# Input projection weights of the second sequence split into high and low parts by transfers from GpSimd's queue

## The chip, the cores and the metric

The kernel runs on one core of one Trainium2 chip. The metric is the device time of one execution in microseconds; the time before is the median of three runs. One further execution was taken with the hardware profiler, and the views quoted here come from it. Engine names: PE is TensorE (matmuls; PEld its weight loads), DVE is VectorE, ACT is ScalarE, POOL is GpSimd, SP is SyncE.

## What is computed

One encoder layer is applied to two inputs, a sequence of 512 tokens and one of 1024, each of width 1024. A normalized input is projected by one wide matrix `w_in` into everything that the two token mixers need; the mixers' outputs are gated, merged and projected, and a SwiGLU FFN follows. Cut to what matters here:

```python
h = rms_norm(x, n_pre_mix)
proj = h @ w_in
qkv_g, z_g, a_g, b_g, q_h, f_h, i_h, g_h, gate_raw = jnp.split(proj, IN_SPLITS, axis=-1)
...
o_a = gated_delta_chunked(q, k, v, g[0], beta[0]) + flip_seq(gated_delta_chunked(...))
o_b = gla_chunked(qh, kh[0], ih, logf[0]) + flip_seq(gla_chunked(...))
...
merged = gates[:, :, 0] * y_a + gates[:, :, 1] * y_b
x = x + rms_norm(merged @ w_out, n_post_mix)
h2 = rms_norm(x, n_pre_ffn)
ff = (jax.nn.silu(h2 @ w_gate) * (h2 @ w_up)) @ w_down
return x + rms_norm(ff, n_post_ffn)
```

All is float32. Both sequences use the same weights.

## The kernel before

**Precision by parts.** A float32 product is made of three TensorE products in the shorter format `float32r`: every operand is written as a high part (the value rounded to `float32r`) and a low part (the value less the high part), and `mm3` adds high x high, high x low and low x high in one PSUM bank. So every weight that arrives must first be split. `split` (line 836) does it with two instructions: ACT copies the raw weights to the high part, and DVE subtracts the high part from the raw ones and writes the low part.

**Input weights.** `w_in` is cut into blocks of 128 output columns, 512 KB each, laid out as 128 partitions x 1024 values. `fetch` (line 1268) loads a block from SP's queue into a raw tile of the general work space (pool `big`), `split_w` makes the two parts in a pair of slots of the weight pool (`NW` slots of 1024 values; 6 before), and `in_w` (line 1263) joins the two. The blocks used by a sequence are q, k and v of the delta-rule mixer for four heads, six blocks a head for the other mixer and the branch gates z and G (`dense`), and 16 blocks of the merging gates (`gates`). `proj` (line 1233) multiplies one block with one 512-token block of the input in 24 matmuls of 128 x 512; the first sequence has one such token block, the second has two.

**Order of the work.** The kernel's text isn't issued as it stands. Generators for the parts of the layer (`pre_stream`, `gdn_stream`, `hg_stream`, `dense_stream`, `p2_stream`) are interleaved by a first planner (`Plan.run`), which walks TensorE's time; `TOKENS` and `NORMED` are planner times at which the start's normalization may go on, and `take_w` and `give_w` hold two weight tokens. The operations that come out are recorded on a `Tape`, and `Tape.schedule` puts them in order a second time for each engine: it charges each an occupancy (`occ`) and a duration (`dur`) by `Tape.cost`, adds `SLACK` to results that cross from one engine to another, allows eight transfers in flight (`LANES`), looks at most `AHEAD` = 500 operations ahead of the earliest one unfinished, gives out tiles as they come free, and prefers operations that `sooner` has moved forward. What comes out is a fixed order of instructions for each engine's queue; on the chip the engines wait for each other by semaphores alone.

**POOL's own work in the second sequence.** `inverse` (line 1339) runs 31 steps of two small operations, each needing the one before, on POOL; its result goes through a scratch tensor in DRAM to `merges`, whose small matmuls (32 x 32, then 64 x 64) PE does; then `gdn_mix` steps through the recurrence. POOL issues no transfers.

Of the kernel before, what the change touches and what calls it, by code (L numbers as in the profile page):

```python
# [33 lines left out]
C_Z, C_A, C_QH, C_FH, C_IH, C_GH, C_GATE = 1536, 2048, 2064, 2576, 3600, 4112, 4624  # L34
QSCALE = 128.0 ** -0.5
TBUFS = 8
NW = 6
NH = NFF // 2
MIXER = ("ones", "offd", "m_all", "m_b", "mbd", "wab0", "wab1")
RBUFS = 1  # L40
# [7 lines left out]
NVEC = 88  # L48
AHEAD = {0: 1536, 1: 2064, 4: 4112 - 512}
TRIG = 2  # L50
TOKENS, NORMED = 10.0, 30.0
QSQ = P * EPS ** 0.5
EPSQ = P * EPS * EPS

# [108 lines left out]
class Tape:  # L163
# [12 lines left out]
    AHEAD = 500  # L176
    RATE = 260.0
    FETCH = 5000.0
    BLOCK = 256
    SLACK = {"sync": 600, "vector": 100, "scalar": 100, "gpsimd": 100, "tensor": 100}  # L180

# [106 lines left out]
    def cost(self, o, out, ins, scal):  # L288
        e, m = o.eng, o.meth
        n = self.free_size(out)  # L290

        def psum(a):
            v = self.vts.get(a.tensor.name)
            return v is not None and v.pool.kind == "PSUM"
        if m == "dma_start":
            vo = self.vts.get(out.tensor.name)
            run = self.row(out, ins[0])
            rows = out.shape[0] * n // run
            o.form = rows * max(run * 4, 512) / self.RATE
            if vo is None or vo.pool.kind == "DRAM":  # L300
                o.dur = 1200.0
            elif [x for x in ins[0].ap if x[0] == 0 and x[1] > 1]:
                o.dur = 4000.0
            else:
                o.dur = 2000.0
            o.occ = 380.0 if rows < 512 else 450.0
            if o.dur < 2000.0 and run < P:
                o.occ = 600.0
            return
        if e == "tensor":  # L310
            if m == "transpose":
                o.occ = 110
                o.form = self.FULL
            else:
                k = self.free_size(ins[1])
                form = (ins[0].shape[0], self.free_size(ins[0]))
                if ins[1].dtype == F32R:
                    o.occ = k / 2.4 + 13.5
                else:
                    o.occ = 2 * (2 * k / 2.4 + 5.5) if k > 32 else 24  # L320
                    o.form = form
                    if form == (64, 64):
                        o.occ = 62
                    elif form == (P, 32) and k > 32:
                        o.occ = 32 if k <= 64 else k / 2.4 + 3
            o.dur = o.occ + 165
            return
        if e == "scalar":
            d = 200 + 0.84 * self.free_size(ins[0]) - (45 if psum(ins[0]) else 0) + 92 * len(scal)
            o.dur, o.occ = d, d - (95 if o.kw.get("accum_out") is None else 0)  # L330
            return
        if e == "vector":
            ps = psum(out) or any(psum(i) for i in ins)
            if not ps and m != "memset" and (m != "tensor_scalar" or n > 1):
                o.port = 138 + 65 * len(scal)
            if m == "tensor_tensor_scan":
                d = 155 + 1.98 * n
            elif m in ("tensor_copy", "tensor_scalar", "memset") and not ps:
                d = 145 + 0.53 * n
            else:  # L340
                d = 145 + 1.055 * n
            if m in ("copy_predicated", "transpose"):
                d += 30
            d += 65 * len(scal)
            o.dur, o.occ = d, d - 75
            return
        if m == "memset":
            d = 90 + 0.86 * n
        elif m == "affine_select":
            d = 100 + 1.05 * n  # L350
        else:
            d = 192 + (1.87 if n < TB else 2.15) * n
        if m != "memset":
            o.port = 138
        o.dur, o.occ = d, d - 40
# [79 lines left out]
    def schedule(self):  # L435
# [33 lines left out]
        def lat(a, b):  # L469
            a, b = self.ENGS[a], self.ENGS[b]  # L470
            return self.LAT.get((b, a), 30 if a == b else 36)
# [22 lines left out]
        def enable(o, t):  # L494
            o = o.unit[0]
            npend[o.idx] -= 1
            o.rel = max(o.rel, t)
            if npend[o.idx] == 0:
                ask(o)
# [14 lines left out]
        while done < len(ops):  # L514
# [69 lines left out]
            for o in o.unit:  # L584
                start[o.idx] = (t, done)
                turn[o.idx] = (first, done)
                for v in o.tiles:
                    if v.pool.kind == "PSUM":
                        v.use[e] = t + o.dur
                done += 1  # L590
                clock[e] = t + o.occ
                fin = t + o.dur
                for s in o.succ:
                    if s.eng == e == "tensor":
                        enable(s, t + o.occ)
                    else:
                        enable(s, fin + lat(e, s.eng) + (self.SLACK[e] if e != s.eng else 0))
                for v in o.tiles:
                    if v.left == len(v.ops):
                        v.fin = {}  # L600
                    v.left -= 1
                    v.fin[e] = max(v.fin.get(e, 0.0), fin)
                    if v.left == 0:
                        v.pool.give(v)
                        if v.pool not in freed:
                            freed.append(v.pool)
                t += o.occ
# [157 lines left out]
def layer(ctx, tc, x_p, x_s, w_out, n_post_mix, n_post_ffn, w_down, vec, xt_p, xt_s, w_in, w_br, w_gate, w_up,  # L765
# [196 lines left out]
    def whl():  # L962
        return [pl.tile(wsp, [P, 1024], F32R, n, n, WBUFS[i]) for i, n in enumerate(("whi", "wlo"), 1)]

    def split_w(raw, kt, m):
# [3 lines left out]
            split(hi[:, 0:n], lo[:, 0:n], raw[:, 0:n])  # L969
        return [v[:, 0:n].rearrange("p (k m) -> p k m", m=m) for v in (hi, lo)]  # L970

    def get_w(src, kt, m):
        raw = raw_w()
        if kt * m == src.shape[1]:
            dma(raw, src)
        else:
            dma(raw.rearrange("p (k m) -> p k m", m=m), src.rearrange("(k p) m -> p k m", p=P))
        return split_w(raw, kt, m)
# [281 lines left out]
                give_w()  # L1260
            yield 0

    def in_w(c0):
        return split_w(ahead.pop(c0) if c0 in ahead else fetch(c0), KD, P)

    ahead = {}
# [99 lines left out]
    def gdn_in(q, h, out):  # L1366
        nb = q.nb
        out.update({"ktok": {}, "vtok": {}, "q2": {}, 0: {}, 1: {}, "D": {}, "vc": {}, "nrm": {}})
        yield take_w(True)
        w = in_w(512 + h * P)  # L1370
        for b in range(nb):
            for d in range(2):
                dm = gt_("at", 4)
                dma(dm, q.cr[4 * d + h:4 * d + h + 1, b * TB:(b + 1) * TB].to_broadcast([P, TB]))
                sg = 1 if d == 0 else -1
                nc.gpsimd.affine_select(t4(dm), t4(dm), [[0, 4], [sg, P]], ALU.is_ge, NEG, base=0,
                                        channel_multiplier=-sg)
                pl.op("POOL", dm, [dm])
                out["D"][b, d] = dm
        yield pl.at(w[1])  # L1380
        yield from conv_proj(q, h, 1, w, out)
        while out["post"]:
            yield from out["post"].pop(0)

    def qv_in(q, h, out):
        for pi in (0, 2):
            yield take_w(True)
            w = in_w(pi * 512 + h * P)
            yield pl.at(w[1])
            yield from conv_proj(q, h, pi, w, out)  # L1390

# [325 lines left out]
    def dense_stream():  # L1717
        for q in seqs:
            lists = [list(dense(q)), list(gates(q))]
            yield need(("h", q.si, 0))  # L1720

            def pick():
                for l in lists:
                    if l and need(*l[0][0])() is not None:
                        return l.pop(0)
                return None

            def avail():
                for l in lists:
                    if l and need(*l[0][0])() is not None:  # L1730
                        return 0.0
                return None
            cur = None
            while lists[0] or lists[1] or cur:
                if cur is None:
                    yield avail
                    yield take_w(False)
                    it = pick()
                    cur = (it, in_w(it[1]))
                    yield None  # L1740
                nxt = None
                if tok["w"] and not tok["want"] and avail() is not None:
                    tok["w"] -= 1
                    it = pick()
                    nxt = (it, in_w(it[1]))
                it, w = cur
                yield from proj(q, w, it[2])
                if it[3] and waiting:
                    waiting.append(lambda k=it[3]: pl.mark(k))
                elif it[3]:  # L1750
                    pl.mark(it[3])
                cur = nxt
            pl.mark(("dense", q.si))
# [875 lines left out]
```

## Time and profile before

| | |
|---|---|
| median of 3 runs | 2383.68 us (2383.06 to 2385.79) |
| the profiled execution, whole | 2382.66 us |
| its span, first to last instruction | 2381.0 us |
| transfers | 337.72 MB, mean 142 GB/s |
| reads of HBM | 254.59 MB |

The profile gives the busy time of each engine, and for a stretch of time the same by engine. An operation's row ends with the engine's idle time just before it and what ended that. The chain of waits goes back from the last instruction: at each step to what released it, or to the instruction before it on its engine. Matmuls are pipelined, and the profile lets one last until its result is out, so neighbours overlap; the pace is counted by how many start in a stretch.

### The profile page before, as it was taken

The numbers are of one execution on the slowest core, as the hardware profiler recorded it, in microseconds if no ns is written. First come the engines' busy times: TensorE is split into PE (matmuls) and PEld (weight loads), VectorE is DVE, ScalarE is ACT, GpSimd is POOL, SyncE is SP. The second block draws the span as 40 slices with busy tenths as digits, with TensorE's granted clock in tenths as the row PEclk, the third lists the DMA queues.
The fourth block names the chain that finished last, engine by engine and source line by source line (L and its number), as shares of the span: only waits on it lengthen the run. The fifth ranks groups of instructions, "written<-read, shape, count | busy, mean of one in ns | idle before, by whom it ended". The sixth has DMA issues, their size and how long they took to land.

```text
span 2381.0 us, 37933 instructions
## 1 busy us (share of the span) xinstructions
PE 2362.8 (99%) x14183; PEld 1974.6 (83%) x14183; DVE 1727.0 (73%) x2826; ACT 1239.0 (52%) x2159; POOL 755.4 (32%) x1019
## 2 busy tenths in 40 slices
PE   8999999999999999999999999999999999999998
PEld 7888888888888888888888888888888888888887
DVE  8777898857857968758766984755887877544566
ACT  6656776746637547548442464545354444433343
POOL 0623435241602612502310011114666774200221
PEclk9999999999999999999999999999999999999999
DMA  5242643221330321324873463552454544674463
GB/s 199 95 145 63 218 143 101 95 66 46 101 96 18 100 83 54 96 78 148 299 261 133 159 221 110 163 170 84 168 192 175 187 170 160 213 246 137 148 206 125
DMA packets 193496, 337.72 MB, mean 142 GB/s; under 512 B 53185, under 2 KB 92961, under 8 KB 193313
## 3 DMA queue, kind: packets, MB, share of 16 engines
q1 hardware_dynamic: 193312, 335.31, 42.6%
q8 instruction: 111, 1.82, 0.3%
q14 instruction: 73, 0.59, 0.1%
HBM read 254.59 MB, written 80.66 MB: 141 GB/s over the span
## 4 chain that ended last, share of the span: by engine, by line
PE 90%; DVE 2%; DMA 1%; ACT 1%; SPq 0%; issue 0%; POOL 0%; DVEq 0%; ACTq 0%; POOLq 0%
PE bank L649 90%; DVE la_a L649 1%; DMA ba_a<-lay_w_in 1%; DVE ba_a L649 1%; ACT la_a L649 0%; SPq L649 0%; DMA ba_a<-x_sample 0%; DVE wa_a L649 0%; ACT ba_a L649 0%; ACT wa_a L649 0%; DMA dram_g_sc<-la_a 0%; ACT sm_a L649 0%; DMA la_a<-dram_u_sc 0%; DVE sm_a L649 0%; POOL la_a L649 0%
## 5 line engine op out<-in xcount | busy, mean ns | idle before, releaser
L649 PE MATMUL bank<-ha_a,wa_a 128*128 128x512 f32 x5424 | 1307.7, 395 | 8.4 <-ACT wa_a L649 8.0
L649 PEld LDWEIGHTS bank<-ha_a,wa_a 128*128 128x128 f32 x5424 | 1003.7, 188 | 210.1 <-ACT wa_a L649 8.0
L649 PE MATMUL bank<-xr_a 128*128 128x512 f32 x1386 | 314.3, 389 | 0.0
L649 PEld LDWEIGHTS bank<-xr_a 128*128 128x128 f32 x1386 | 260.1, 188 | 54.0
L649 PE MATMUL bank<-xr_a,ha_a 128*128 128x512 f32 x1200 | 275.3, 389 | 0.0
L649 PEld LDWEIGHTS bank<-xr_a,ha_a 128*128 128x128 f32 x1200 | 225.2, 188 | 46.8
L649 POOL TENSOR_TENSOR ba_a<-ba_a 128x512 f32<-128x512 f32 (+1 forms) x123 | 159.8, 1305 | 219.0 <-ACT wa_a L649 79.9
L649 ACT ACTIVATE la_a<-la_a 128x512 f32<-128x512 f32 (+1 forms) x307 | 194.4, 649 | 42.5 <-DVE la_a L649 30.7
L649 DVE TENSOR_TENSOR wa_a<-la_a,wa_a 128x1024 fp32r<-128x1024 f32 (+1 forms) x121 | 142.0, 1184 | 59.7 <-PE bank L649 28.3
L649 ACT ACTIVATE wa_a<-la_a 128x1024 fp32r<-128x1024 f32 (+1 forms) x121 | 118.3, 986 | 106.2 <-PE bank L649 97.7
L649 DVE TENSOR_TENSOR wa_a<-ba_a,wa_a 128x1024 fp32r<-128x1024 f32 (+1 forms) x103 | 123.6, 1218 | 68.7 <-PE bank L649 57.5
L649 ACT ACTIVATE wa_a<-ba_a 128x1024 fp32r<-128x1024 f32 (+1 forms) x103 | 99.3, 980 | 118.5 <-PE bank L649 94.9
L649 ACT ACTIVATE ha_a<-ba_a 128x512 fp32r<-128x512 f32 (+1 forms) x126 | 80.7, 642 | 135.7 <-PE bank L649 109.9
L649 POOL TENSOR_TENSOR la_a<-la_a 128x256 f32<-128x256 f32 (+1 forms) x80 | 89.4, 1133 | 183.1 <-DVE la_a L649 67.9
L649 DVE TENSOR_TENSOR ha_a<-ba_a,ha_a 128x512 fp32r<-128x512 f32 (+1 forms) x126 | 127.9, 1020 | 13.4 <-ACT ha_a L649 12.8
L649 DVE TENSOR_TENSOR la_a<-la_a 128x512 f32<-128x512 f32 (+2 forms) x193 | 126.2, 669 | 12.6 <-ACT la_a L649 11.6
L649 POOL TENSOR_TENSOR la_a<-la_a,sm_a 128x30 f32<-128x30 f32 (+43 forms) x248 | 124.6, 502 | 18.3
L649 POOL TENSOR_TENSOR sm_a<-la_a 128x126 f32<-128x126 f32 (+37 forms) x155 | 79.8, 515 | 133.2 <-DMA la_a<-dram_u_sc 104.4
L649 PE MATMUL bank<-wa_a,ha_a 128*128 128x512 f32 x528 | 120.1, 389 | 0.0
L649 DVE TENSOR_TENSOR xr_a<-da_a,xr_a 128x1024 fp32r<-128x1024 f32 (+2 forms) x60 | 71.2, 1200 | 64.1 <-ACT xr_a L649 44.0
L649 ACT ACTIVATE ba_a<-ba_a 128x512 f32<-128x512 f32 (+1 forms) x164 | 104.6, 648 | 24.0 <-DVE ba_a L649 16.7
L649 PEld LDWEIGHTS bank<-wa_a,ha_a 128*128 128x128 f32 x528 | 99.0, 188 | 20.5
(205 smaller groups left out, 3305.0 us busy)
## 6 DMA issues: line engine op xcount, KB each, us to landing
la_a<-lay_w_in SPq DMA_DIRECT2D x67, 512.0 KB
ba_a<-lay_w_in SPq DMA_DIRECT2D x37, 512.0 KB
ba_a<-lay_w_gate SPq DMA_DIRECT2D x35, 512.0 KB
ba_a<-lay_w_up SPq DMA_DIRECT2D x34, 512.0 KB
dram_a_sc<-xa_a SPq DMA_DIRECT2D x56, 256.0 KB
ba_a<-w_ffn_down SPq DMA_DIRECT2D x24, 512.0 KB
da_a<-dram_a_sc SPq DMA_DIRECT2D x22, 512.0 KB
ba_a<-dram_a_sc SPq DMA_DIRECT2D x20, 512.0 KB
```

Of the source, the lines that this page charges most:

```text
L649: f(*[m(a) for a in o.args], **{k: m(a) for k, a in o.kw.items()})
```

## The change

For the second sequence (`q.si` is 1) `in_w` no longer loads raw weights and splits them. `cast_w` issues a transfer from POOL's queue that casts the weights from DRAM to `float32r` in the high tile; ACT writes minus the high part to the low tile; and a second transfer from POOL's queue adds the weights from DRAM to the low tile. No raw tile and no DVE instruction is left. These operations are moved forward by `CAST` = 150 places (the split had `URGENT` = 100).

Beside that, the weight pool gets 8 slots for 6, `TOKENS` is 14 for 10, the second planner charges a transfer from POOL 1300 ns of POOL's time and 2600 ns plus its bytes (twice for one that adds), and it adds the slack of SP's transfers behind every transfer, those whose user is on the same queue too.

```diff
-NW = 6
+NW = 8
+CAST = 150
-TOKENS, NORMED = 10.0, 30.0
+TOKENS, NORMED = 14.0, 30.0
+    ISSUE = 1300.0
...
+            if e == "gpsimd":
+                o.dur = 2600.0
+                o.occ = self.ISSUE
+                if o.kw:
+                    o.form *= 2
+                return
...
-                        enable(s, fin + lat(e, s.eng) + (self.SLACK[e] if e != s.eng else 0))
+                        enable(s, fin + lat(e, s.eng) + (self.SLACK["sync" if o.meth == "dma_start" else e] if e != s.eng or o.meth == "dma_start" else 0))
...
+    def cast_w(src):
+        hi, lo = whl()
+        with nc.sooner(CAST):
+            nc.gpsimd.dma_start(hi, src)
+            pl.dma(hi, src)
+            act(lo, hi.bitcast(F32), AF.Copy, scale=-1.0)
+            nc.gpsimd.dma_start(lo, src, accum_op=ALU.add)
+            pl.dma(lo, src)
+        return [v.rearrange("p (k m) -> p k m", m=P) for v in (hi, lo)]
...
-    def in_w(c0):
+    def in_w(q, c0):
+        if q.si:
+            return cast_w(w_in[(c0 if c0 < C_A else c0 - (C_QH - C_A)) // P])
         return split_w(ahead.pop(c0) if c0 in ahead else fetch(c0), KD, P)
```

The four calls of `in_w` pass `q` along.

More of the change, by code (lines that the diff above doesn't have):

```diff
@@ L1369, in gdn_in @@
         yield take_w(True)
-        w = in_w(512 + h * P)
+        w = in_w(q, 512 + h * P)
         for b in range(nb):
@@ L1387, in qv_in @@
             yield take_w(True)
-            w = in_w(pi * 512 + h * P)
+            w = in_w(q, pi * 512 + h * P)
             yield pl.at(w[1])
@@ L1738, in dense_stream @@
                     it = pick()
-                    cur = (it, in_w(it[1]))
+                    cur = (it, in_w(q, it[1]))
                     yield None
@@ L1744, in dense_stream @@
                     it = pick()
-                    nxt = (it, in_w(it[1]))
+                    nxt = (it, in_w(q, it[1]))
                 it, w = cur
```

## The prediction

> **What bounds the kernel now.** I read the page's first part, then the stages, then TensorE's waits, then the chain that ended last.
>
> ```profile
> span 2381.0 us, 37933 instructions
> PE 2362.8 (99%) x14183; PEld 1974.6 (83%) x14183; DVE 1727.0 (73%) x2826; ACT 1239.0 (52%) x2159; POOL 755.4 (32%) x1019
> ```
>
> TensorE (PE) lacks 18.2 us of being busy all the time. Where these lie is shown by the stages: 0 to 390 us is the first sequence's mixer, 390 to 1060 us the second sequence's projections, recurrences and gates, where the changed weights are used, 1060 to 1662 us the merge and the first part of the FFN, and the rest the FFN's end. The columns are PE, weight loads, VectorE (DVE), ScalarE (ACT), GpSimd (POOL), the granted clock, the transfer engines' busy share and GB/s.
>
> ```profile
> 0.00:390.00 390.00, 379.91 (x2759) 315.09 (x2760) 315.88 (x598) 266.76 (x486) 157.81 (x359) 1.00 0.41 137
> 390.00:1060.00 670.00, 669.31 (x5252) 567.68 (x5251) 500.14 (x967) 386.90 (x734) 212.20 (x382) 1.00 0.27 80
> 1060.00:1662.00 602.00, 602.00 (x3038) 502.97 (x3037) 418.75 (x657) 292.69 (x479) 99.77 (x91) 1.00 0.51 173
> 1662.00:2381.00 719.00, 711.55 (x3140) 588.85 (x3138) 492.23 (x605) 292.69 (x463) 285.62 (x188) 1.00 0.52 176
> ```
>
> In the stage that the change is about, PE is idle for 670.00 - 669.31 = 0.69 us. The idle time of the whole kernel is 10.09 us before 390, 0.69 us here and 7.45 us at the end, behind the last matmul. PE's waits, and the last pieces of the chain, say the same:
>
> ```profile
> PE bank L649 <- ACT wa_a L649: 9.1, 4, 8.0
> PE bank L649 <- DVE la_a L649: 0.6, 1, 0.6
> PE bank L649 <- DVE wa_a L649: 0.4, 1, 0.4
> ...
> 404.38 240.51 PE bank L649 x1749
> 644.90 182.99 PE bank L649 x1329
> 827.93 1545.63 PE bank L649 x7897
> 2373.59 0.70 DVE da_a L649
> ```
>
> One wait of 8.0 us is the start; from 404.38 to 2373.56 the chain is PE, with two pieces of about 0.01 and 0.04 us missing between. The clock is 1.00 in every stage. So the kernel is bound by TensorE's own work, and no weight of the second sequence is waited for. What the change relieves (DVE) is busy 500.14 of 670 us and holds nothing up for long.
>
> **What it removes.** Each sequence uses 4 x 9 + 16 = 52 input weights (q, k, v and six dense blocks a head, and 16 gate blocks), so half of the 67 + 37 loads below go:
>
> ```profile
> L649 SPq DMA_DIRECT2D la_a<-lay_w_in x67: 327/423/1607, 1.7 to 1021.4; - x67
> L649 SPq DMA_DIRECT2D ba_a<-lay_w_in x37: 328/423/1336, 12.8 to 1020.4; - x37
> L649 DVE TENSOR_TENSOR wa_a<-la_a,wa_a 128x1024 fp32r<-128x1024 f32 x34 | 42.6, 1262 | 15.2 <-ACT wa_a L649 10.0 <-PE bank L649 5.2
> L649 DVE TENSOR_TENSOR wa_a<-ba_a,wa_a 128x1024 fp32r<-128x1024 f32 x13 | 16.4, 1271 | 7.3 <-PE bank L649 6.3 <-DMA la_a<-dram_w_sc 0.9
> L649 ACT ACTIVATE wa_a<-la_a 128x1024 fp32r<-128x1024 f32 x35 | 37.1, 1060 | 32.1 <-PE bank L649 29.1 <-DMA la_a<-lay_w_in 3.0
> ```
>
> (The last three rows are of 390 to 1060 us.) 52 issues of 0.42 us leave SyncE's queue, 22 us, and what stood behind them there can go earlier; 52 subtractions of 1.26 us leave DVE, 66 us; the raw tiles leave the work space. On PE's path this is worth at most the stage's 0.69 us. ACT keeps its 52 operations of 1.06 us: the copy to the high part becomes a negation of the same shape.
>
> **What it adds.** 104 transfers issued on POOL's queue, which has issued none so far, so their cost has no row. The nearest is SyncE's issue, 0.33 to 1.61 us: 104 of them take 34 to 167 us of a POOL that is free for 670 - 212.20 = 458 us. I take 1.3 us, which the new planner assumes, 135 us in all; it lies inside these ends.
>
> The transfers also move twice the bytes: 52 x 0.52 MB = 27 MB more over 670 us, 41 GB/s on top of 80. What PE does beside much more is shown by the first row here; the second gives PE's plain pace, 60 us / 266 = 0.2256 us a matmul.
>
> ```profile
> 1140.00:1200.00 60.00, 60.00 (x288) 50.44 (x287) 49.48 (x61) 24.41 (x37) 21.70 (x13) 1.00 0.80 277
> 1320.00:1380.00 60.00, 60.00 (x266) 49.70 (x265) 51.04 (x59) 25.16 (x30) 0.00 (x0) 1.00 0.47 153
> ```
>
> At 277 GB/s PE misses nothing, so the extra traffic costs nothing.
>
> **How late a weight comes.** It is now load, negate, add the load, one after the other. A lone load (issued at 735.74; nothing moves from 739 on, so it takes under 3.3 us) and the slowest piece of the chain bound one transfer:
>
> ```profile
> 735.74 0.38 SPq L649 DMA_DIRECT2D la_a<-lay_w_in  x1
> ...
> 739.00:741.00 2.00, 2.00 (x11) 1.65 (x10) 2.00 (x3) 2.00 (x5) 1.57 (x5) 1.00 0.00 0
> ...
> 246.16 7.99 DMA ba_a<-x_sample
> ```
>
> Low: 2 x 3.3 + 1.06 + 2 x 0.42 = 8.5 us. High: 2 x 7.99 + 1.06 + 2 x 1.61 = 20.3 us. Against this stands what PE has in hand. A weight feeds 2 blocks x 24 = 48 matmuls, 48 x 0.2256 = 10.8 us, and in this stage one is used up every 670 / 52 = 12.9 us. With 8 slots (NW) there is room for four pairs: three weights ahead, 32 us, beat 20.3; and four slots turn over in (20.3 + 10.8) / 4 = 7.8 us a weight, beneath 12.9. So lateness is hidden by the projections already loaded, at either end of the range. Without that cover each weight would cost up to 20.3 us, 52 times. I take 0.
>
> **Who queues behind the new waits.** The negation waits at the head of ACT's queue for the cast to land; behind it stand evictions of PSUM, and behind those PE, with eight banks of 5.4 us (24 x 0.2256) each. ACT is free for 283 of 670 us. The adding transfer waits on POOL for the negation; behind it stands the 32-step inverse of the delta rule, whose result PE's merges need. This is where it can go wrong, and is priced below.
>
> **The planner's other edits.** Instructions are put in order by a planner at build time, so NW, the later start of the norms (TOKENS 14), the 0.6 us added behind every transfer and the priorities move instructions, and add none. Ahead of 390 us they could win the idle 10.09 us less the start's 8.0, 2.1 us, and at the start
>
> ```profile
> 6.40 0.61 ACT L649 ACTIVATE la_a<-la_a 128x512 f32<-128x512 f32 x1
> 6.92 1.04 ACT L649 ACTIVATE wa_a<-la_a 128x1024 fp32r<-128x1024 f32 x1
> ```
>
> the 0.6 us of a square that ACT runs ahead of the first weight's copy. They could as well lose as much in a new order; later norms keep more projections waiting in PSUM. I take 0 between -2.7 and +2.7.
>
> **The sum.** The profiled execution took 2382.66 us, its span 2381.0 and 1.66 around it; the median, 2383.68, lies 1.02 above. On PE: nothing added, nothing removed, at most 0.69 us of waits gone. From the median: 2383.68 - 0.69 = 2383.0 us. A measurement of this kernel can tell about 0.2%, 4.8 us, from no change, so this is "the same".
>
> **Rival 1: slower, POOL holds up the inverse.** Before, for one head of the second sequence and for one of the first (POOL's first and last operation of an inverse, then PE's first merge; POOL's last, then PE's merge):
>
> ```profile
> 459.82 0.40 POOL L649 TENSOR_TENSOR sm_a<-la_a 128x31 f32<-128x31 f32 x1 [40.19 <-DMA la_a<-dram_u_sc]
> 494.96 0.24 POOL L649 TENSOR_TENSOR la_a<-la_a,sm_a 128x16 f32<-128x16 f32 x1
> ...
> 509.33 0.21 PE L649 MATMUL bank<-la_a,ba_a 32*32 32x32 f32 x1
> ...
> 107.67 0.21 POOL L649 TENSOR_TENSOR la_a<-la_a,sm_a 128x8 f32<-128x8 f32 x1
> ...
> 116.59 0.21 PE L649 MATMUL bank<-ba_a,la_a 32*32 32x32 f32 x1
> ```
>
> The inverse takes 35.4 us, and PE's merge comes 14.1 us behind it, where 8.7 sufficed in the first sequence: 5.4 us to spare. Into 35.4 us fall 35.4 / 12.9 = 2.7 weights, 5.5 issues. The new order allows 1.3 us for each; PE's order is fixed, so PE stands still once POOL loses 5.4 / 5.5 = 1.0 us more on each, that is from 2.3 us an issue. At 3.0 us the loss is (3.0 - 2.3) x 5.5 = 3.9 us a head, 15.4 us in four: 2399. For it speaks that POOL's operations do stretch beside a busy DVE, two of one shape here by three:
>
> ```profile
> 410.84 2.03 POOL L649 TENSOR_SCALAR_AFFINE_SELECT ba_a<-ba_a 128x512 f32<-128x512 f32 x1 [4.51 <-DMA ba_a<-dram_cr_sc]
> 413.52 0.68 POOL L649 TENSOR_SCALAR_AFFINE_SELECT la_a<-la_a 128x512 f32<-128x512 f32 x1 [0.65 <-DMA la_a<-dram_cr_sc]
> ```
>
> 1.3 us stretched by 2.03 / 0.68 would be 3.9. Against it: DVE has 66 us less to do, and a planner that reckons with a longer POOL also moves the merges back. The same loss would come from casts that land later than planned, with the addition stuck behind them.
>
> The Trainium skill, page "SBUF — State Buffer", speaks against the change: by its section "Who interferes with whom", a transfer issued from GpSimd has its descriptors written by GpSimd, which cannot write them while VectorE runs a copy or scalar operation in its two-port mode; its section "A bandwidth-pool intuition that's wrong" has such a transfer at 3.1 us in place of 0.62. By that, on every issue, the sum would be (3.1 - 2.3) x 5.5 x 4 = 17.6 us above no change, about 2401, an estimate from that page. But the operations it names are few in the stage; the largest such group is
>
> ```profile
> L649 DVE TENSOR_SCALAR la_a<-la_a,sa_a 128x512 f32<-128x512 f32 x22 | 12.4, 562 | 0.0
> ```
>
> 12.4 of 670 us, 2% of the time; by that share the rule would hit 2 of 104 issues and leave the time where it is. No row here shows an issue from POOL.
>
> **Rival 2: faster.** The visible waits give 0.69 + 2.1 + 0.6 = 3.4 us, 2380.3, still within 0.2%. More must come out of PE's busy time, from changes between full matmuls and small ones:
>
> ```profile
> 1033.73 4.37 PE L649 MATMUL bank<-ha_a,wa_a 128*128 128x512 f32 x18
> 1038.04 0.27 PE L649 MATMUL bank<-ba_a 64*64 64x64 f32 x1
> ```
>
> 18 matmuls take 4.31 us, where 18 x 0.2256 = 4.06: a change costs 0.25 us. An order with 16 fewer of them gives 4 us more, 2376.3. For it: weights that are ready early and a freer DVE leave the planner more full matmuls to choose from. Against it: the changes follow the steps of the merges and the recurrence, which stay.
>
> **Rival 3: the change doesn't do what it says.** If the cast left the raw bits as they are, the low part would be raw minus raw, and the same instructions would run in the same time; this belongs to the forecast's case.
>
> **Numbers.** The forecast, PE bound and all of it hidden: 0.58. Rival 1 or its like, slower by over 4.8 us: 0.26. Rival 2, faster by over 4.8 us: 0.16. The likeliest time is 2383.0. The range goes to rival 2's 2376 and rival 1's 2399, the price at 3.0 us an issue; I leave out some 0.07 below and 0.10 above, where POOL loses still more. The forecast's own range is 2380.3 to 2386.4 (0.69 and 2.7 us either way).
>
> **What would show it.** Right: PE at 669 or more of 670 us in the second sequence's stage; 52 loads fewer on SyncE; POOL with 104 issues of about 1.3 us; DVE about 66 us less busy in all; ACT unchanged; PE's waits still led by the start's 8 us. Wrong: PE idle ahead of the 32 x 32 merges with POOL as the releaser (rival 1), or on a transfer into the weight tiles (a chain longer than 32 us); or a PE busy time below 2360 us (rival 2). The forecast falls if PE's idle time outside the two ends exceeds 7 us.

## The result, and the profile after

The changed kernel takes 2392.62 us (median of 7 runs, 2391.13 to 2396.2), the kernel before 2384.05 us in runs beside them (7 runs, 2382.88 to 2385.79): 1.0037 times as long, 95% interval 1.0025 to 1.0049. So it is slower by some 9 us, where "the same", 2383.0, was forecast; 2392.62 lies inside the range. The profiled execution took 2392.4 us.

The page of after, its span, its busy times and the row of POOL's issues; then the stages, in the columns of before:

```profile
span 2390.7 us, 37932 instructions
PE 2365.8 (99%) x14183; PEld 1975.5 (83%) x14183; DVE 1667.5 (70%) x2773; ACT 1240.4 (52%) x2159; POOL 793.8 (33%) x1123
...
L657 POOL DMA_DIRECT2D wa_a<-lay_w_in x104 | 77.0, 748 | 302.3 <-PE bank L657 147.8
...
wa_a<-lay_w_in POOLq DMA_DIRECT2D x104, 512.0 KB, 5.5
...
la_a<-lay_w_in SPq DMA_DIRECT2D x36, 512.0 KB, 4.9
```

```profile
390.00:1060.00 670.00, 663.37 (x5206) 561.23 (x5205) 441.24 (x915) 384.09 (x727) 248.48 (x477) 1.00 0.49 114
1060.00:1662.00 602.00, 600.55 (x3037) 501.55 (x3036) 411.92 (x649) 286.90 (x470) 104.13 (x95) 1.00 0.53 179
1662.00:2390.70 728.70, 721.32 (x3183) 597.14 (x3181) 498.87 (x614) 300.15 (x475) 288.49 (x189) 1.00 0.51 174
```

The span is 9.7 us longer. PE's idle time went from 18.2 to 24.9 us, and its busy time from 2362.8 to 2365.8 us (2361.9 us in the kernel below that has no holds). The idle time is new in two places: 6.63 us in the second sequence's stage, where it was 0.69, and 1.45 us in the next, where it was none. What the change was to do, it did: DVE is busy 59.5 us less, and POOL issues 104 transfers. PE's waits, and pieces of the chain that ended last in the stretch that had been all PE:

```profile
PE bank L657 <- ACT wa_a L657: 9.4, 3, 8.0
PE bank L657 <- DVE la_a L657: 3.6, 3, 2.9
PE bank L657 <- issue: 1.3, 1, 1.3
PE bank L657 <- ACT la_a L657: 1.2, 2, 1.0
```

```profile
513.96 5.46 DVE ba_a L657 x5
520.97 1.66 DVE la_a L657 x2
522.76 49.96 PE bank L657 x429
...
1088.03 1.77 DVE la_a L657 x5
1089.83 3.89 DVE la_a L657 x2
1095.76 228.32 PE bank L657 x1272
```

The start's 8.0 us is as before. What is new is a wait of 2.9 us for DVE, an engine that has less work than before. The chain names the place: five DVE operations from 513.96 take 5.46 us. The instructions there, in order of time (DVE's, then POOL's, then PE's; the value behind the start is the length):

```profile
515.66 3.70 DVE L657 TENSOR_TENSOR_SCAN ba_a<-sm_a,ba_a 128x128 f32<-128x128 f32 x1
519.28 0.66 DVE L657 TENSOR_TENSOR ba_a<-la_a,ba_a 128x512 f32<-128x512 f32 x1
...
514.66 1.45 POOL L657 DMA_DIRECT2D wa_a<-lay_w_in  x2
515.83 0.93 POOL L657 TENSOR_SCALAR_AFFINE_SELECT la_a<-la_a 128x512 f32<-128x512 f32 x1
516.42 0.92 POOL L657 TENSOR_SCALAR_AFFINE_SELECT ba_a<-ba_a 128x512 f32<-128x512 f32 x1
517.02 0.89 POOL L657 TENSOR_TENSOR la_a<-la_a 128x256 f32<-128x256 f32 x1
517.60 1.48 POOL L657 TENSOR_SCALAR_AFFINE_SELECT la_a<-la_a 128x512 f32<-128x512 f32 x2
519.51 0.91 POOL L657 TENSOR_TENSOR ba_a<-ba_a 128x256 f32<-128x256 f32 x1 [0.44 <-DVE ba_a L657]
...
522.76 0.64 PE L657 MATMUL bank<-la_a 32*32 32x32 f32 x39 [2.91 <-DVE la_a L657]
```

One scan of 128x128 lasts 3.70 us; 28 others of that shape, on other tiles, take 0.41 on average (all 66 others between 390 and 1130 us: 0.44). It starts while POOL's two issues run, and ends when POOL, after two issues and five operations with no gap between them, comes to its first idle time (the 0.44 us ahead of 519.51). Behind it in DVE's queue stands what PE's 32 x 32 merge needs, and PE idles 2.91 us.

Such places can be counted: DVE operations between 390 and 1130 us that last over 1 us longer than the lower quartile of their shape ("held" from here on). Before has none; its largest excess is 0.46 us. After has six, with 11.9 us of excess together: at 398.54, 515.66, 598.03, 749.55, 917.74 and 1090.43 us. Five of them start within 1.4 us of an issue from POOL; of these, four end when POOL's run does, and the one at 398.54 ends in the middle of POOL's run, as its next issue ends. The sixth, at 598.03, is the smallest (1.19 us, 1.03 too long). It starts 6.8 us behind the last issue, and POOL had a gap of 2.74 us in between, so an issue doesn't explain it. Before has runs of POOL operations as long and as tight (four additions from 1073.01 to 1078.24, without a gap), and beside them no DVE operation loses over 0.43 us.

### The profile page after: what moved, and what is told of

The parts are those of the page before. It is cut to its first block, busy times and chain, and to the rows that moved or that the text cites. A ratio compares the mean times of both kernels' runs of the same rounds, so it can differ in the third digit from the quotient of the medians.

```text
span 2390.7 us, 37932 instructions
## 1 busy us (share of the span) xinstructions
PE 2365.8 (99%) x14183; PEld 1975.5 (83%) x14183; DVE 1667.5 (70%) x2773; ACT 1240.4 (52%) x2159; POOL 793.8 (33%) x1123
## 4 chain that ended last, share of the span: by engine, by line
PE 90%; DVE 5%; ACT 2%; DMA 2%; issue 1%; SPq 0%; POOL 0%; DVEq 0%; POOLq 0%; ACTq 0%
PE bank L657 90%; DVE la_a L657 2%; DVE ba_a L657 2%; ACT la_a L657 1%; ACT ba_a L657 1%; DVE sm_a L657 1%; DMA la_a<-lay_w_in 0%; ACT wa_a L657 0%; DMA la_a<-x_sample 0%; DMA la_a<-dram_u_sc 0%; DMA la_a<-dram_cr_sc 0%; DVE wa_a L657 0%; DMA dram_g_sc<-ba_a 0%; SPq L657 0%; ACT sm_a L657 0%
## 5 line engine op out<-in xcount | busy, mean ns | idle before, releaser
L657 POOL TENSOR_TENSOR ba_a<-ba_a 128x512 f32<-128x512 f32 (+1 forms) x130 | 170.9, 1323 | 218.2 <-DVE ba_a L657 54.6
L657 POOL DMA_DIRECT2D wa_a<-lay_w_in x104 | 77.0, 748 | 302.3 <-PE bank L657 147.8
L657 ACT ACTIVATE ha_a<-ba_a 128x512 fp32r<-128x512 f32 (+1 forms) x134 | 86.5, 650 | 147.2 <-PE bank L657 118.2
L657 ACT ACTIVATE wa_a<-ba_a 128x1024 fp32r<-128x1024 f32 (+1 forms) x88 | 81.6, 944 | 123.1 <-PE bank L657 119.7
L657 DVE TENSOR_TENSOR ha_a<-ba_a,ha_a 128x512 fp32r<-128x512 f32 (+1 forms) x134 | 134.2, 1007 | 13.3 <-ACT ha_a L657 13.2
L657 DVE TENSOR_TENSOR wa_a<-la_a,wa_a 128x1024 fp32r<-128x1024 f32 (+1 forms) x84 | 96.9, 1163 | 54.4 <-issue 22.9
L657 DVE TENSOR_TENSOR wa_a<-ba_a,wa_a 128x1024 fp32r<-128x1024 f32 (+1 forms) x88 | 98.2, 1119 | 35.8 <-PE bank L657 27.5
L657 ACT ACTIVATE wa_a<-la_a 128x1024 fp32r<-128x1024 f32 (+1 forms) x84 | 80.9, 977 | 65.5 <-PE bank L657 57.6
L657 ACT ACTIVATE xr_a<-da_a 128x1024 fp32r<-128x1024 f32 (+2 forms) x60 | 58.5, 987 | 106.0 <-PE bank L657 105.8
L657 POOL TENSOR_TENSOR sm_a<-la_a 128x28 f32<-128x28 f32 (+32 forms) x155 | 69.9, 451 | 130.9 <-DMA la_a<-dram_u_sc 120.4
```

Of the source, the lines that this page charges most:

```text
L657: f(*[m(a) for a in o.args], **{k: m(a) for k, a in o.kw.items()})
```

## The experiments

**Theory.** From the moment POOL issues a transfer, a DVE operation on SBUF can lose its turn and wait until POOL next has a gap; without an issue the two take turns, one operation each. Where POOL has a run of work behind an issue, DVE stands still for all of it, and in this kernel PE then waits for DVE. **Rivals:** the new order (slots, TOKENS, slack) costs the time; the weights land too late; the planner's wrong price of an issue, 1.3 us for a measured 0.75, packs POOL's work too tightly.

The table holds all kernels of the layer; each ratio is to runs of before on the same chip. Held and idle are those of the one profiled execution; idle is PE's, in us, in the stages 390 to 1060 and 1060 to 1662.

| kernel | median us | to before, 95% interval | held | idle |
|---|---|---|---|---|
| before | 2384.05 | | 0 | 0.69, 0.00 |
| after | 2392.62 | 1.0037 (1.0025 to 1.0049) | 6 | 6.63, 1.45 |
| planners' edits alone | 2383.52 | 0.9998 (0.9989 to 1.0007) | 0 | 2.43, 0.00 |
| transfers alone | 2392.91 | 1.0035 (1.0021 to 1.0049) | 5 | 6.34, 0.93 |
| issue at 650 ns | 2390.39 | 1.0024 (1.0015 to 1.0034) | 6 | 6.97, 0.94 |
| transfers earlier | 2393.13 | 1.0040 (1.0027 to 1.0054) | 4 | 6.29, 0.93 |
| gap, buffers moved | 2392.44 | 1.0039 (1.0026 to 1.0052) | 0 | 1.51, 0.52 |
| no gap, buffers moved | 2401.83 | 1.0073 (1.0061 to 1.0086) | 5 | 6.37, 1.56 |
| before, buffers moved | 2393.94 | 1.0040 (1.0024 to 1.0055) | 0 | 0.19, 0.00 |
| gap, buffers in place | 2382.07 | 0.9991 (0.9982 to 1.0000) | 0 | 1.20, 0.52 |
| no gap, buffers in place | 2390.66 | 1.0029 (1.0017 to 1.0040) | 6 | 5.77, 1.57 |
| gap in place, 1000 ns | 2386.26 | 1.0008 (0.9999 to 1.0017) | 0 | 1.99, 1.06 |

**Which half of the change.** The planners' edits alone:

```diff
-NW = 6
+NW = 8
-TOKENS, NORMED = 10.0, 30.0
+TOKENS, NORMED = 14.0, 30.0
...
-(self.SLACK[e] if e != s.eng else 0)
+(self.SLACK["sync" if o.meth == "dma_start" else e] if e != s.eng or o.meth == "dma_start" else 0)
```

> The planners' edits alone (8 weight slots, TOKENS 14, the longer slack behind transfers); the weights are split by ACT and DVE as before, and POOL issues no transfer. First theory (POOL's issues hold DVE back): no DVE operation between 390 and 1130 us is stretched by over 1 us, and the time stays within 3 us of before, about 2384. Rival (the new order itself costs the time): about 2392, with PE idle some 5 us or more between 390 and 1060.

And the transfers alone, which is after with these three lines put back:

> The transfers from POOL alone, with 6 weight slots, TOKENS 10 and the old slack rule. First theory (POOL's issues hold DVE back): several DVE operations stretched by over 1 us again, 2389 to 2396. Rival (the new order of slots and slack costs the time): within 3 us of before, about 2384. Third theory (the weights land too late through POOL's queue): with fewer slots the loads start later, so more than after, over 2395, with PE waiting for ACT or POOL on the weight tiles.

The edits alone give 2383.52 us, no hold, and the time of before. The transfers alone give all of the loss, 2392.91 us with five holds. The planners' edits as a cause fall. The transfers bring an order of their own, though; the gap trial below keeps that order and settles it. Lateness in the form it was given falls too, as fewer slots cost nothing on top. A kernel with after's order and the 104 transfers issued from SyncE was planned but has no measurement, so in the layer itself the issuing queue alone was never exchanged.

**The hold by itself.** A kernel of stages: both engines start together, DVE runs 24 small additions, POOL issues a transfer and runs six additions.

```python
nc.gpsimd.dma_start(hi, src)
for r in range(24):
    nc.vector.tensor_tensor(dv[r % 2], da, db, ALU.add)
for r in range(6):
    nc.gpsimd.tensor_tensor(pv[r % 2], pa, pb, ALU.add)
```

> Nothing of the layer is computed; ten short stages, each with 24 DVE additions of 128x128 beside 6 POOL additions of 128x256 without a gap, ahead of which stand: nothing, a casting transfer from POOL, the same and a small memset, a plain transfer, an adding one, two casting ones, a casting one and a wait for DVE, a casting one with no additions behind it, one between the second and third addition, and a transfer from SP. First theory, form a (any run of POOL without a gap holds DVE): in all stages with six additions, that with no transfer too, one DVE addition lasts as long as the run, 4 us or more. Form b (an issue from POOL makes it): with no transfer and with SP's no DVE addition lasts over about 1.3 us, one POOL addition and its own 0.3; in the stages with an issue just ahead one lasts to the end of the run, 3 to 5 us; behind the wait none. Rival (DVE is not held by POOL's issues): no addition over 1.3 us in any stage.

The DVE addition that stands beside POOL's run, in the stage with no transfer, with a first casting one, with a plain one, and with one between the second and third addition:

```profile
3.18 0.81 DVE L102 TENSOR_TENSOR dv<-da,db 128x128 f32<-128x128 f32 x1
...
12.46 0.85 DVE L102 TENSOR_TENSOR dv<-da,db 128x128 f32<-128x128 f32 x1
...
32.87 4.74 DVE L102 TENSOR_TENSOR dv<-da,db 128x128 f32<-128x128 f32 x1
...
81.83 3.38 DVE L102 TENSOR_TENSOR dv<-da,db 128x128 f32<-128x128 f32 x1
```

With no transfer the engines take turns: each DVE addition waits for one POOL addition, 0.81 us. The stage meant for a transfer from SyncE, at 90 us, shows the same 0.81, but it doesn't test SyncE: nothing made the transfer wait for its stage, and it was issued at the very start of the kernel.

```profile
0.74 0.38 SPq L93 DMA_DIRECT2D hi<-lay_w_in  x1
```

With an issue from POOL in the run one DVE addition waits for all that is left of it: 4.74 us for six additions, 3.38 for four, 5.05 behind an adding transfer, 4.58 where a small memset stands between. That is form b. Two stages went against the expectation: the first casting transfer, whose issue took 0.70 us where the later single casting and plain ones took 0.57, and the two issues in a row held nothing over 1 us. So a hold is likely behind an issue, not certain. The second kernel of stages repeated it and tried what ends it:

> Nothing of the layer is computed; fourteen short stages as in the other kernel of stages, each with 24 DVE operations on 128x128 beside POOL additions of 128x256: a first transfer, two casting transfers with 6 additions behind each, one with a single addition, then with one thing put between the issue and the 6 additions (two small operations of which the second needs the first; a small POOL copy that reads the first DVE result; a memset of 128x512; a drain of POOL), then with other DVE operations (scan, copy, scalar multiplication, addition from PSUM), then two issues in a row, then eight small memsets ahead of the issue. Theory (an issue makes DVE lose its turn until POOL leaves a gap): the two plain repeats hold one DVE addition for about 4.7 us, the single addition about 1.3, the read of the DVE result and the drain none over 1.3 us, the memset 5 us; the scan is held as the addition is, the addition from PSUM not. Rival (it was an accident of the first kernel): no operation over 1.3 us, or the same with and without the gap.

One row each, in this order: a plain repeat's run on POOL; the single addition; the memset and the copy that needs it; the small read of DVE's result; the scan; POOL behind the drain; POOL behind eight memsets and the issue.

```profile
13.77 4.12 POOL L113 TENSOR_TENSOR pv<-pa,pb 128x256 f32<-128x256 f32 x6
...
34.43 1.35 DVE L102 TENSOR_TENSOR dv<-da,db 128x128 f32<-128x128 f32 x1
...
42.62 0.81 DVE L102 TENSOR_TENSOR dv<-da,db 128x128 f32<-128x128 f32 x1
...
51.56 4.39 DVE L102 TENSOR_TENSOR dv<-da,db 128x128 f32<-128x128 f32 x2 [0.60 <-POOL tiny L104]
...
82.06 4.73 DVE L94 TENSOR_TENSOR_SCAN dv<-da,db 128x128 f32<-128x128 f32 x1
...
75.87 1.22 POOL L113 TENSOR_TENSOR pv<-pa,pb 128x256 f32<-128x256 f32 x1 [3.45 <-issue]
...
131.21 3.27 POOL L113 TENSOR_TENSOR pv<-pa,pb 128x256 f32<-128x256 f32 x1
```

Both plain repeats held one addition for 4.73 us, as long as the issue and POOL's run. A single addition behind the issue costs 1.35 us, as the length of the run says. A scan, a copy and a multiplication by a scalar are held as an addition is; an addition from PSUM isn't, though its other operand and its result are in SBUF. A memset of 128x512 between does not help, and a second issue doesn't either (4.72 us). Two small operations of which the second waits for the first do: 0.81 us, turns are taken again. The read of DVE's result was expected to help and did not: that result had long been there, so POOL had no gap, and the next addition was held (4.39 us with its successor). Behind the drain DVE is free, but POOL stands for 3.45 us. And where DVE's stream had been running for a while, it was POOL's first addition that waited, 3.27 us to the stream's end: the loser can be either engine.

**The planner's price, and the weights' lateness.** In after, `ISSUE = 650.0` for 1300.0, and in another kernel `CAST = 300` for 150:

> After, with the second planner charging POOL 650 ns for an issue, about the measured time, in place of 1300. Theory (DVE is held by chance wherever a POOL run stands behind an issue, whatever the plan's price): the places move, some DVE operations over 1 us stay, 2387 to 2395. Rival (the wrong price makes the runs, and with them the loss): no such operation, 2383 to 2386.

> After, with the transfers and their ACT step moved forward by 300 places in the second planner in place of 150, so that the weights come earlier. Theory (held DVE): the places move, the loss stays, 2388 to 2395. Rival (the weights land too late): PE's waits on the weight tiles in the second sequence go, 2383 to 2387.

2390.39 and 2393.13 us: the places move (six holds and four), the loss stays. The lower price is 2.2 us faster by the medians, but the intervals of the ratios overlap. The second kernel says little of lateness: its transfers were issued only 0.6 us earlier in the median. What speaks against lateness is the trace of after itself, where PE has no wait for a weight tile between 390 and 1060 us.

**A gap behind every issue.** After's order, and behind each of the 104 issues two small POOL operations, the second of which needs the first; in the control the copy reads another tile, `gap[2]`, and nothing else differs.

```diff
             f(*[m(a) for a in o.args], **{k: m(a) for k, a in o.kw.items()})
+            if o.eng == "gpsimd" and o.meth == "dma_start":
+                self.nc.gpsimd.memset(self.gap[0], 0.0)
+                self.nc.gpsimd.tensor_copy(self.gap[1], self.gap[0])
```

> After's order unchanged, but behind each of the 104 issues POOL runs a memset of 128x8 and a copy of 128x8 that needs it, which leaves POOL a gap (in the kernel of stages this let DVE in at once). Theory (DVE loses its turn from an issue to POOL's next gap): no DVE operation between 390 and 1130 us stretched by over 1 us, the PE idle time between 390 and 1060 falls from 6.6 to 3 us or less, 2384 to 2388, in spite of some 50 us more work on POOL. Rival (the loss is POOL's or the weights' lateness): more work on POOL makes it slower than after, 2392 to 2397.

> The control: the same two POOL operations behind each issue, but the copy reads another tile, so that neither waits for the other and POOL has no gap. Theory (DVE loses its turn until POOL's next gap): several DVE operations over 1 us stay, 2390 to 2397. Rival (any delay behind the issue helps, or the gap does nothing): the same time as with the gap, within 2 us.

With the gap no hold is left and PE's idle time in the stage falls from 6.63 to 1.51 us, as the theory has it; but the time is 2392.44 us, as long as after. The control has its holds and takes 2401.83, 9 us more than after. Both lose 10 to 11 us in a new place, the end of the kernel, which the change doesn't touch. The three tiles of 32 bytes stood ahead of all others, so that every buffer on the left side of SBUF had moved by 96 bytes. To tell that from the added operations, before was run with the empty 96 bytes alone:

```diff
+    arena(ctx, "gap", 24, F32)
     sa = arena(ctx, "sa", ends[0], F32)
```

> Before, with 96 bytes of unused SBUF ahead of all buffers of the left side and nothing else. If the place of the buffers made the two gap trials slower: matmuls between 1640 and 2070 us at 232 ns, 2392 to 2395. If it was the added POOL operations: the same as before, within 2 us.

It takes 2393.94 us. The stretch from 1660 to 2060 us of before and then of this kernel:

```profile
1660.00:2060.00 400.00, 400.00 (x1767) 331.20 (x1766) 321.09 (x381) 180.01 (x293) 248.56 (x164) 1.00 0.50 172
```

```profile
1660.00:2060.00 400.00, 400.00 (x1723) 323.96 (x1722) 309.59 (x368) 177.78 (x291) 248.80 (x165) 1.00 0.47 164
```

PE is busy throughout and its clock full in both, but starts 1723 matmuls where it started 1767: 232 ns each for 226. That is the place of the buffers, and not the gap. So both kernels were run again with the three tiles at the far end of the right side, where they move nothing:

> The memset and the copy that needs it behind each issue again, with their three small tiles at the far end of the right side of SBUF, so that no other buffer moves (in the first trial they stood ahead of all others and moved every buffer of the left side by 96 bytes, and the matmuls between 1640 and 2070 us took 232 ns in place of 227). Theory (DVE loses its turn from an issue to POOL's next gap): no DVE operation between 390 and 1130 us over 1 us beyond its usual length, PE idle 1.5 us between 390 and 1060 as in the first trial, matmuls at 227 ns to the end, 2381 to 2385. Rival (the DVE holds cost PE nothing in the end, the loss is elsewhere): 2389 to 2393 still.

> The control with the tiles at the same far end: the same two operations without a wait between them. Theory: the holds stay, 2390 to 2394. Rival: within 2 us of the kernel with the gap.

With the gap 2382.07 us, 0.9991 of before (0.9982 to 1.0000); without it 2390.66. The two differ in one operand of a copy, and by 8.6 us. PE's idle time in the two stages differs by 5.6 us, and its busy time by 3.2, together 8.8. The busy times with the gap and without; the two stages with the gap and then without:

```profile
PE 2361.9 (99%) x14183; PEld 1974.6 (83%) x14183; DVE 1654.8 (70%) x2773; ACT 1239.2 (52%) x2159; POOL 842.7 (35%) x1332
...
PE 2365.1 (99%) x14183; PEld 1975.5 (83%) x14183; DVE 1666.6 (70%) x2773; ACT 1239.0 (52%) x2159; POOL 822.7 (34%) x1332
```

```profile
390.00:1060.00 670.00, 668.80 (x5270) 568.54 (x5269) 436.79 (x929) 387.39 (x736) 297.04 (x673) 1.00 0.49 114
1060.00:1662.00 602.00, 601.48 (x3019) 501.77 (x3018) 415.39 (x646) 291.73 (x478) 107.21 (x104) 1.00 0.53 180
...
390.00:1060.00 670.00, 664.23 (x5214) 562.28 (x5213) 440.82 (x918) 383.02 (x727) 272.29 (x666) 1.00 0.49 114
1060.00:1662.00 602.00, 600.43 (x3032) 501.21 (x3031) 411.88 (x648) 286.14 (x469) 106.66 (x104) 1.00 0.53 179
```

For the kernel with the gap, PE's waits, the chain, and POOL and DVE at the place that was shown for after:

```profile
PE bank L657 <- ACT wa_a L657: 9.5, 3, 8.0
PE bank L657 <- issue: 1.0, 1, 1.0
PE bank L657 <- DVE ba_a L657: 0.5, 1, 0.5
```

```profile
421.29 201.44 PE bank L657 x1409
622.74 691.28 PE bank L657 x4632
1314.08 2.50 DVE ba_a L657 x4
```

```profile
515.40 0.56 POOL L657 DMA_DIRECT2D wa_a<-lay_w_in  x1
515.95 0.13 POOL L659 MEMSET gap_a<- 128x8 f32 x1
516.14 0.52 POOL L660 COPY gap_a<-gap_a 128x8 f32<-128x8 f32 x1
...
515.92 0.68 DVE L657 TENSOR_TENSOR la_a<-la_a 128x512 f32<-128x512 f32 x1
516.52 0.71 DVE L657 STREAM_TRANSPOSE la_a<-la_a 128x512 f32<-128x512 f32 x1
```

The gap is 0.06 us, from 516.08 to 516.14, and it is now the copy that waits for DVE. In the control the addition at this place was held for as long as POOL's run, though POOL executes the same instructions:

```profile
515.93 4.73 DVE L657 TENSOR_TENSOR la_a<-la_a 128x512 f32<-128x512 f32 x1
```

PE's waits for `la_a` from DVE are gone, and the chain is PE from 421 to 1314 us again. The two small operations cost POOL 29.0 and 34.4 us of time that nobody waits for. A last kernel joined the gap to a lower price in the planner, `ISSUE = 1000.0`:

> The kernel with the gap at the far end, and the second planner charging POOL 1000 ns for an issue with its gap (0.57 for the issue and about 0.5 for the two small operations) in place of 1300. Theory (with the holds gone the plan's price matters little): no hold over 1 us, 2380 to 2385, the same as with 1300 within 2 us. Rival (the gap helped only with that one order): holds again, 2388 or more.

No hold, as expected, but 2386.26 us, not within 2 us of the 2382.07. PE's idle time in the two stages is 3.05 us in place of 1.72, and its busy time 2364.0 in place of 2361.9. So beside the holds an order of the same instructions is worth some 4 us one way or the other; why this one is the worse isn't settled.

## Why the prediction was wrong

- **What bounds the kernel** held: PE, and the stage had 0.69 us to win. DVE's 66 us less were worth nothing.
- **What it removes** held: 52 loads fewer, DVE 59.5 us less busy. With the gap it is 72.2 (1727.0 - 1654.8); of the 12.7 us between, 11.9 are the excess of the six held operations.
- **What it adds** is where it failed. The step put the price of an issue on POOL's time alone, 104 times 1.3 us of a POOL that is free, and the sum wrote "On PE: nothing added". POOL's own price was even lower, 0.75 us on average, 77.0 in all. But behind an issue POOL's next run of work shuts DVE out, and DVE is one step ahead of PE: that term was 0 and measures 8.6 us (gap against control). The prediction had quoted a row in which POOL's operations stretch beside DVE, and took it for POOL's loss alone; who is late next when DVE waits for POOL was not asked.
- **How late a weight comes** held. From issue to landing a transfer took 5.5 us in the median, inside 3.3 to 7.99, though 12 of the 104 took longer, up to 10.9 us. PE has no wait for a weight tile between 390 and 1060 us, in after or with the gap, so the cover was enough.
- **The planner's other edits** held: 2383.52 us alone, inside 0 +- 2.7 of before.
- **Rival 1** has the sign and not the mechanism, and the range reached 2399 for its sake: that 2392.62 lies inside is luck. It needed 2.3 us an issue, and the merge at 522.76 waits for DVE, with POOL's inverse long done: that ran from 468.37 to 503.17, 34.8 us with five issues inside it, where it took 35.4 before. The 3.1 us that the prediction took from the Trainium skill's page "SBUF — State Buffer", section "A bandwidth-pool intuition that's wrong", were not met: the longest of the 104 issues took 1.12 us. The share of the operations that this rule names was put too low: all copies and scalar operations of DVE from SBUF take 32 us of the stage, 5%, where the largest group alone was counted, 2%; that changes neither the sum nor the outcome. By the Trainium skill's page "SBUF — State Buffer", section "Who interferes with whom", the engine that issues first has the shared ports for the whole instruction, and the other waits. The trace agrees without an issue (0.81 us, one POOL addition), and behind an issue the measurement differs: DVE waited for six.
- The forecast's own test, PE idle for over 7 us outside the two ends, met the case: 6.63 + 1.45 = 8.08.

## What to carry to other kernels

An issue from POOL's queue was not paid by POOL alone here: look at what POOL runs right behind it, and at who waits for the DVE operation beside it. If POOL has a run of work there, make POOL wait once for itself, for instance by two tiny operations that depend on each other; here that turned a loss of 0.3 to 0.4% into the time of before (0.9991 of it, 0.9982 to 1.0000; with another order 1.0008). And when an experiment needs a small buffer, put it where no other buffer moves.

## What the runs showed of the hardware

- Behind an issue DVE can wait for POOL's whole run, and not for one operation: 4.73 us against 0.81 without an issue. Additions, scans, copies and scalar multiplications of DVE on SBUF were all held (4.62 to 4.73 us); additions with one operand in PSUM were not, in the one stage that tried them. What decides whether an issue starts one is open: in the stages three issues or pairs of issues did not (two of them the first of their kernel), and in the control the hold at 515.93 began 1.3 us behind its issue. In after, four of the five holds that start behind an issue ended with POOL's run, the fifth at POOL's next issue; where a gap followed each issue, 0.06 us of it was enough at 516.08.
- Moving the left side's buffers by 96 bytes slowed the matmuls from 1660 to 2060 us from 226 to 232 ns, and before by 10 us, more than the whole change did. Which buffers make it, and why, is open.
- A drain of POOL behind an issue kept POOL idle for 3.45 us.
